# Three modulation vectors of the second layer moved from the first FFN to the second mixer, FFN steps issued one at a time, and one activation-table load instead of three

## The chip, the core and the metric

The kernel runs on one core of one Trainium2 chip. The number that counts is the device time of one execution in microseconds (us); three runs of the kernel before the change are the base. The engines are named as in the profile: PE does the matrix products and PEld loads its weights, DVE is the vector engine, ACT the scalar (activation) engine, POOL a further vector engine that is nearly idle here, and SP issues most of the DMAs.

## What is computed

Two layers of a diffusion backbone over 512 latent and 256 context tokens of width 1024. What matters here:

```python
for l in range(2):
    m_lat = split(silu(c)     @ mod_w[l] + mod_b[l], 6)   # mod_w[l]: 1024 x 6144
    m_ctx = split(silu(c_ctx) @ mod_w[l] + mod_b[l], 6)
    h = modulate(rms(x) , m[0], m[1])                     # shift, scale
    o = _even_mixer(h) if l == 0 else _odd_mixer(h)       # GLA + attention | HGRN2
    x = x + m[2] * rms(o @ w_out)                         # gate
    h = modulate(rms(x), m[3], m[4])
    x = x + m[5] * rms(swiglu(h))                         # hidden width 2816
```

Each layer needs six modulation vectors of 1024 numbers, for the latent and for the context stream. In layer 1 only the latent stream goes on after the mixer, so its vectors 2 to 5 are needed for one stream alone. In the code a vector and stream is written as a pair (m, r): r is 0 for the latents and 1 for the context. Layer 0's mixer has forget gates whose log-sigmoid needs `exp` and `ln` on ACT; layer 1's mixer has learned lower bounds (a softmax over two rows, computed once and early).

## The kernel before

Every float32 operand is split into a high and a low part (`wH`, `wL`; `x` stands for both parts of the activations), and every product is three matmuls (`mm3`, L371). A weight slab of 512 KB goes through a DMA into `raw`, a cast on ACT (`wH`, L698 and L753) and a subtraction on DVE (`wL`, L699 and L754). The order of each engine's instructions is found by the framework's scheduler when the kernel is built, except in parts that are pinned to the order in which they are written (layer 0's mixer and the heads of layer 1's mixer are, the first FFN and the values of the second mixer are not).

**Modulation vectors.** `mod_vec` is a generator that other loops advance. A step loads one slab `mraw` (128 rows of `mod_w` by 1024, 512 KB) and DVE adds it, weighted by one number per row, to an accumulator `macc` (L551 for the first row block, L553 for the other seven); where a job holds a vector for both streams, one slab is added to two accumulators. When a job's eight row blocks are through, four matmuls add up the partitions (`mod_acc`, L371), DVE copies the sums (`modrows`, L485), PE turns them with four transposes (`modT`, L374), and DVE adds the bias (`modcol`, L497). A job with a gate also makes a row of it (`gc` L599, transpose `gcT`, `gt` L605, a small DMA).

**The first FFN** (about 440 to 940 us of the span) runs gate and up projections as a block scheme of seven products (`seven`: the bank `ab` and the tiles `E` and `D` take the results, and DVE folds them into `go` and `uo` at L825, L832, L834, L835), and the down projection in parts (`acc_part`: `acc` is added to `y` at L846). Its function `fill` advances the FFN's modulation generator by one `yield`: twice in every product `seven`, once for every token tile of `acc_part`. That generator (`late_mods`) has five jobs: layer 0's gate 5, layer 1's vectors 0 and 1 (each for both streams), and layer 1's vectors 2 to 5 for the latents.

**The second mixer** begins with the values: x times the part of `odd_w_in` that starts at column 3 D, in column blocks of 256. Two blocks are done while the FFN ends. The other two, c0 = 512 and 768, are the loop at the head of `odd_mixer`; `odd_values` does three pairs of token tiles each (576 `nat` matmuls in all). Then come the heads (`ff` is their first product).

**The activation table.** `gla_gates` runs twice in layer 0's mixer and begins with a request for the table with `exp` and `ln` (L1218). The lower bounds (`lower_bounds`, L454) run before it and cause a load of their own.

Of the kernel before, what the change touches and what calls it, by code (L numbers as in the profile page):

```python
# [18 lines left out]
D = 1024  # L19
# [11 lines left out]
R_C, R_CC, R_NPM, R_MB, R_NQM, R_NPF, R_NQF, R_BG, R_LB, R_GG, R_HG, R_END = 0, 8, 16, 32, 128, 144, 160, 176, 180, 212, 213, 214  # L31
# [102 lines left out]
class Attention:  # L134
# [66 lines left out]
    def turned(self, p, dsts, vector, scratch=False):  # L201

        nc, net = self.nc, self.net
        for b, dst in enumerate(dsts):
            m = dst.shape[1]
            pt = net.sc_tile("pT", self.other()) if b and scratch else net.tr_tile("pT")
            for i in range(m):
                net.tr(pt[:, i * P : (i + 1) * P], p[:, (4 * b + i) * P : (4 * b + i + 1) * P], net.ident)
            src = pt[:, : m * P].rearrange("p (c i) -> p c i", c=m)
            (nc.vector.tensor_copy if b in vector else nc.scalar.copy)(dst, src)  # L210
# [19 lines left out]
    def rows(self, t):  # L230
        nc, net = self.nc, self.net
        pr = net.tr_tile("rB")
        for j in range(4):
            for n in range(2):
                hd = 4 * n + j
                net.mm(
                    pr[self.half[n], P * j : P * j + P],
                    self.r[t][:, hd : hd + 1].to_broadcast([P, 64]),
                    net.ident,
                    start=True,  # L240
                    stop=True,
                    tile_position=(0, 64 * n),
                )
        w = net.wp.tile([P, WU], F32, tag="mraw", bufs=2, name="o")
        nc.scalar.copy(w[:, :512], pr)
        self.o[t] = w[:, :512], w[:, 512:]
# [93 lines left out]
class Net:  # L340
# [187 lines left out]
        yield  # L528
        turned()

    def mod_vec(self, pool, jobs, own=None, bufs=2, sums=2):


        nc = self.nc
        steps = [(l, k, m) for l, ms, _ in jobs for k in range(KD) for m in sorted({m for m, _ in ms})]
        load = lambda l, k, m: self.mod_loads(l, (m,), k, own, bufs)[0]
        u = load(*steps[0])
        i = 0
        for l, ms, then in jobs:
            self.mod_tiles(l, [m for m, r in ms if r == 0])  # L540
            accs = [pool.tile([P, D], F32, tag="macc", bufs=sums, name=f"macc{l}{m}{r}") for m, r in ms]
            while i < len(steps) and steps[i][0] == l and steps[i][2] in [m for m, _ in ms]:
                k, m = steps[i][1:]
                i += 1
                ahead = load(*steps[i]) if i < len(steps) else None
                for a, (mm, r) in zip(accs, ms):
                    if mm != m:
                        continue
                    w = self.scT[:, k, r : r + 1]
                    if k == 0:  # L550
                        nc.vector.tensor_scalar(a, u, w, None, op0=ALU.mult)  # L551
                    else:
                        nc.vector.scalar_tensor_tensor(a, u, w, a, op0=ALU.mult, op1=ALU.add)  # L553
                u = ahead
                yield

            yield
            acc = self.tr_tile("mod_acc")
            for j in range(4):
                self.mm(  # L560
                    acc[32 * j : 32 * j + 32, :],
                    self.one.to_broadcast([P, 32]),
                    accs[j // 2][:, (j % 2) * 512 : (j % 2) * 512 + 512],
                    start=True,
                    stop=True,
                    tile_position=(0, 32 * j),
                )
            turned = self.mod_cols(l, acc, 512, [(m, r, 0, 2 * n, 0, 2) for n, (m, r) in enumerate(ms)])
            yield
            turned()  # L570
            if then:
                rows = self.gate_rows(l, *then)
                yield
                rows()
# [482 lines left out]
    def even_mixer(self, h, mix, zu, last):  # L1057
        nc, I = self.nc, self.I
        w = I["even_w_in"][0]
# [32 lines left out]
        def decays():  # L1092
# [7 lines left out]
            for c in range(2):  # L1100
                yield from self.gla_gates(mixg, tp, c, zT, wg, fs[c])

        self.lower_bounds()
        mods = self.mod_vec(tp, ((0, ((2, 0), (2, 1)), (2, R_NQM)), (0, ((3, 0), (3, 1)), None)), tp, 3, 4)

# [109 lines left out]
    def gla_gates(self, mixg, tp, c, zT, wg, fs):  # L1215

        nc = self.nc
        self.tc.keep_in_program_order(nc.scalar.preload_act_table_set("natural_log_exp_and_others"))  # L1218
        for t0, N in ((SEQ, CTX), (0, SEQ)):
            f = mixg.tile([P, 2, N], F32, tag=f"glaf{c}{t0}", bufs=1, name=f"glaf{c}{t0}")  # L1220
            for d in range(2):
                bias = self.col[:, R_BG + 2 * d + c : R_BG + 2 * d + c + 1]
                pt = self.sc_tile(f"logit{c}{d}")[:, :N]
                self.mm(pt, wg[:, d, c * P : (c + 1) * P], zT[:, t0 : t0 + N], start=True, stop=True)
                am = tp.tile([P, 2, SEQ], F32, tag="am", bufs=2, name="am")
                a, m = am[:, 0, :N], am[:, 1, :N]
                nc.scalar.activation(a, pt, AF.Abs, bias=bias)
                nc.scalar.activation(a, a, AF.Exp, scale=-1.0)
                nc.scalar.activation(a, a, AF.Ln, bias=self.one)
                nc.vector.tensor_scalar(m, pt, bias, 0.0, op0=ALU.add, op1=ALU.min)  # L1230
                nc.vector.tensor_tensor(m, m, a, op=ALU.subtract)
                nc.scalar.activation(f[:, d, :], m, AF.Exp, scale=1.0 / 16.0)
                if d:
                    fs.append(f)
                yield
# [96 lines left out]
    def odd_mixer(self, h, fi):  # L1332
        nc, I = self.nc, self.I
        w = I["odd_w_in"][0]
        for c0 in range(512, D, 256):
            self.odd_values(fi, h, c0, (4, 0, 2))

        with self.pool("hg") as gp:
            ones = gp.tile([P, CTX], F32, tag="ones", name="ones")
# [283 lines left out]
    def run(self):  # L1623
        nc, I, out = self.nc, self.I, self.out
# [17 lines left out]
        h = Split(ha)  # L1642
        with self.pool("pre0") as pp:
# [18 lines left out]
            for half in range(2):  # L1662
# [26 lines left out]
                for r, tok in ((1, slice(512, 768)), (0, slice(0, 512))):  # L1689
                    for k in range(ks.start, ks.stop):  # L1690
                        x = xT[:, k, tok]
# [52 lines left out]
        def late_mods(pool):  # L1744
            return self.mod_vec(
                pool,
                (
                    (0, ((5, 0), (5, 1)), (5, R_NQF)),
                    (1, ((0, 0), (0, 1)), None),
                    (1, ((1, 0), (1, 1)), None),  # L1750
                    (1, ((2, 0), (3, 0)), (2, R_NQM, 1)),
                    (1, ((4, 0), (5, 0)), (5, R_NQF, 1)),
                ),
            )

        def ending(ys):
# [19 lines left out]
            return ender(ep, 0, 5, order, xat(x1), only_lat(xat(x2)), (1, 1, 0, R_NPM), h1), values(), ep  # L1776

        ys = self.ffn(0, ha, yp, fp, pp, rp, forms, ending, late_mods)
        fp.release()

# [73 lines left out]
```

## Time and profile before

| | |
|---|---|
| median of 3 runs | 1752.65 us (1751.57 to 1753.44) |
| the profiled execution | 1750.86 us, of which the span of the core is 1749.1 us |
| granted PE clock, mean | 0.994 |
| PE busy | 1700.5 us, 97% of the span |
| PEld busy | 1524.9 us, 87% |
| DVE busy | 1276.7 us, 73% |
| ACT busy | 858.2 us, 49% |
| DMA | 187.23 MB, mean 107 GB/s |

The span is the time from the first to the last recorded instruction; 1.76 us of the profiled execution lie around it. PE works almost all the time, so what a change gains or costs is to be looked for in the moments in which PE does not work, and in the work that it is given.

### The profile page before, as it was taken

The page shows a single profiled execution, that of the slowest core. Times are in us where ns is not written, and L with a number is a line of the kernel's source. Part 1 is how long each engine was busy: PE and PEld are TensorE (multiplying, and loading weights), DVE is VectorE, ACT ScalarE, POOL GpSimd, SP SyncE. Part 2 cuts the span into 40 slices and gives each one's busy share as a digit, 9 for nine tenths or more (in the row PEclk, how much of TensorE's full clock was granted, in tenths as well). Part 3 has the DMA queues.
Part 4 walks back from the last instruction along what each step waited for, and adds up shares of the span by engine and source line. Part 5 has one row for each costly group of instructions (what it writes and reads, how often), then busy time and mean ns, then how long its engine had stood idle before and what let it go on. Part 6 is the DMA issues. An engine that isn't in the chain of part 4 may idle for free. (4 is left out here: it accounts for less than half of the span.)

```text
span 1749.1 us, 32748 instructions
## 1 busy us (share of the span) xinstructions
PE 1700.5 (97%) x13720; PEld 1524.9 (87%) x13720; DVE 1276.7 (73%) x2035; ACT 858.2 (49%) x1475; POOL 74.0 (4%) x93
## 2 busy tenths in 40 slices
PE   6999999999999999999999999999999999999998
PEld 4888986778998889898998998889898898899997
DVE  5879658735969999796668328787764678878785
ACT  5545557736542233333346436666644654444342
POOL 1004100001000000000001000000000000000000
PEclk8999999999999999999999999999999999999999
DMA  8731013154324465452225222121124333233333
GB/s 318 221 112 39 3 38 107 34 156 141 119 85 145 133 192 170 134 179 61 73 85 180 85 61 63 48 62 50 50 62 133 121 103 99 88 107 105 94 106 120
DMA packets 169647, 187.23 MB, mean 107 GB/s; under 512 B 6262, under 2 KB 140956, under 8 KB 169500
## 3 DMA queue, kind: packets, MB, share of 16 engines
q1 hardware_dynamic: 167568, 181.56, 33.0%
q10 hardware_dynamic: 1932, 3.59, 0.6%
q8 instruction: 107, 1.75, 0.4%
q14 instruction: 40, 0.33, 0.1%
HBM read 175.66 MB, written 9.46 MB: 106 GB/s over the span
## 5 line engine op out<-in xcount | busy, mean ns | idle before, releaser
L699 DVE TENSOR_TENSOR wL<-raw,wH 128x1024 fp32r<-128x1024 f32 (+1 forms) x126 | 151.3, 1207 | 115.7 <-ACT wH L698 115.4
L371 PE MATMUL nat<-wH,x 128*128 128x256 f32 (+1 forms) x1216 | 228.5, 287 | 0.0
L753 ACT CAST wH<-raw 128x1024 fp32r<-128x1024 f32 x120 | 124.6, 1052 | 176.6 <-PE acc L371 82.8
L371 PEld LDWEIGHTS nat<-wH,x 128*128 128x128 f32 x1216 | 193.2, 193 | 2.3 <-ACT natq L1115 0.8
L754 DVE TENSOR_TENSOR wL<-raw,wH 128x1024 fp32r<-128x1024 f32 x120 | 145.3, 1221 | 62.9 <-ACT wH L753 62.8
L698 ACT CAST wH<-raw 128x1024 fp32r<-128x1024 f32 (+1 forms) x126 | 128.9, 1039 | 113.3 <-PE nat L371 35.8
L371 PE MATMUL nat<-wL,x 128*128 128x256 f32 (+1 forms) x608 | 173.4, 285 | 0.0
L371 PE MATMUL acc<-wH,gH 128*128 128x512 f32 x440 | 172.6, 393 | 0.0
L371 PE MATMUL acc<-wH,gL 128*128 128x512 f32 x440 | 171.7, 390 | 0.0
L371 PE MATMUL acc<-wL,gH 128*128 128x512 f32 x440 | 171.5, 390 | 0.0
L846 DVE TENSOR_TENSOR y<-y,acc 128x1024 f32<-128x1024 f32 x135 | 114.9, 862 | 31.5 <-PE acc L371 28.2
L371 PE MATMUL ff<-x,wH 128*128 128x512 f32 (+1 forms) x512 | 127.6, 340 | 0.0
L553 DVE SCALAR_TENSOR_TENSOR macc<-mraw,scT,macc 128x1024 f32<-128x1024 f32 x98 | 122.6, 1278 | 4.7 <-DMA mraw<-in_mod_w_dram 4.5
L623 POOL TENSOR_TENSOR rs<-ms,neghalf 128x1 f32<-128x1 f32 (+2 forms) x62 | 58.0, 937 | 1597.5 <-DVE ms L621 1597.4
L371 PEld LDWEIGHTS nat<-wL,x 128*128 128x128 f32 x608 | 117.3, 193 | 0.0
L371 PE MATMUL oproj<-wH,x 128*128 128x512 f32 x320 | 102.7, 398 | 2.4 <-ACT x L1269 2.4
L371 PEld LDWEIGHTS acc<-wH,gH 128*128 128x128 f32 x440 | 82.6, 188 | 19.7 <-issue 2.5
L371 PEld LDWEIGHTS acc<-wH,gL 128*128 128x128 f32 x440 | 82.6, 188 | 17.4
L371 PEld LDWEIGHTS acc<-wL,gH 128*128 128x128 f32 x440 | 82.7, 188 | 16.1
L371 PEld LDWEIGHTS ff<-x,wH 128*128 128x128 f32 x512 | 87.3, 190 | 10.0
L954 ACT COPY qkh<-arr 128x512 f32<-128x512 f32 x112 | 70.0, 642 | 36.5 <-DVE arr L959 32.2
L371 PE MATMUL ff<-x,wL 128*128 128x256 f32 (+1 forms) x256 | 86.2, 337 | 0.0
(345 smaller groups left out, 4046.2 us busy)
## 6 DMA issues: line engine op xcount, KB each, us to landing
mraw<-in_mod_w_dram SPq DMA_DIRECT2D x96, 512.0 KB, 4.4
raw<-in_ffn_w_gate_dram SPq DMA_DIRECT2D x44, 512.0 KB, 3.8
raw<-in_ffn_w_up_dram SPq DMA_DIRECT2D x44, 512.0 KB, 3.9
raw<-in_ffn_w_down_dram SPq DMA_DIRECT2D x44, 512.0 KB, 3.6
raw<-in_odd_w_in_dram SPq DMA_DIRECT2D x40, 512.0 KB, 3.8
raw<-in_even_w_in_dram SPq DMA_DIRECT2D x16, 512.0 KB, 4.4
x<-xr SPq DMA_DIRECT2D x14, 512.0 KB, 2.6
xr<-x SPq DMA_DIRECT2D x14, 512.0 KB, 3.6
```

The costliest lines, as they stand in the source:

```text
L371: return self.pin(self.nc.tensor.matmul(*a, **k))
L553: nc.vector.scalar_tensor_tensor(a, u, w, a, op0=ALU.mult, op1=ALU.add)
L623: nc.gpsimd.tensor_tensor(rs, ms, self.neghalf.to_broadcast([P, w]), op=ALU.pow)
L698: nc.scalar.copy(H[:, :m], raw[:, :m])
L699: nc.vector.tensor_tensor(L[:, :m], raw[:, :m], H[:, :m].bitcast(F32), op=ALU.subtract)
L753: self.nc.scalar.copy(H, f)
L754: self.nc.vector.tensor_tensor(L, f, H.bitcast(F32), op=ALU.subtract)
L846: nc.vector.tensor_tensor(y, y, pt, op=ALU.add)
L954: nc.scalar.copy(qkv[:, :, :, half, :], dst)
```

## The change

Four things change.

1. `mod_vec` gets a switch `single`. With it, a row block that is added to two accumulators takes two `yield`s, one for each addition; without it both additions stand in one.
2. The first FFN's generator loses layer 1's vectors 2, 3 and 4 and is run with `single`. It has four jobs instead of five, 32 slab loads instead of 56, 56 additions on DVE instead of 80, and 66 `yield`s instead of 69; `fill` is called 90 times. A job with one vector computes its sums twice over, so it still has four `mod_acc` matmuls.
3. The three vectors are made in `odd_mixer`, among the blocks c0 = 512 and 768 of the values: five `yield`s after each pair of token tiles, with four buffers for slabs and three accumulators in a pool of their own.
4. The request for the table moves from `gla_gates` to the line ahead of `lower_bounds`.

```diff
-    def mod_vec(self, pool, jobs, own=None, bufs=2, sums=2):
+    def mod_vec(self, pool, jobs, own=None, bufs=2, sums=2, single=False):
...
-                for a, (mm, r) in zip(accs, ms):
-                    if mm != m:
-                        continue
+                here = [(a, r) for a, (mm, r) in zip(accs, ms) if mm == m]
+                for x, (a, r) in enumerate(here):
+                    if x and single:
+                        yield
                     w = self.scT[:, k, r : r + 1]
...
-                    accs[j // 2][:, (j % 2) * 512 : (j % 2) * 512 + 512],
+                    accs[j // 2 % len(accs)][:, (j % 2) * 512 : (j % 2) * 512 + 512],
...
+        self.tc.keep_in_program_order(nc.scalar.preload_act_table_set("natural_log_exp_and_others"))
         self.lower_bounds()
...
     def gla_gates(self, mixg, tp, c, zT, wg, fs):
         nc = self.nc
-        self.tc.keep_in_program_order(nc.scalar.preload_act_table_set("natural_log_exp_and_others"))
...
     def odd_mixer(self, h, fi):
+        lp = self.open_pool("late")
+        late = self.mod_vec(lp, ((1, ((2, 0), (3, 0)), (2, R_NQM, 1)), (1, ((4, 0),), None)), lp, 4, 3)
         for c0 in range(512, D, 256):
-            self.odd_values(fi, h, c0, (4, 0, 2))
+            us = self.nat_units(w, 3 * D + c0, 256, 0) + self.nat_units(w, 3 * D + c0, 256, 1)
+            for t0 in (4, 0, 2):
+                self.odd_values(fi, h, c0, (t0,), us)
+                for _ in range(5):
+                    next(late, None)
+        for _ in late:
+            pass
+        lp.release()
...
                     (0, ((5, 0), (5, 1)), (5, R_NQF)),
                     (1, ((0, 0), (0, 1)), None),
                     (1, ((1, 0), (1, 1)), None),
-                    (1, ((2, 0), (3, 0)), (2, R_NQM, 1)),
-                    (1, ((4, 0), (5, 0)), (5, R_NQF, 1)),
+                    (1, ((5, 0),), (5, R_NQF, 1)),
                 ),
+                single=True,
```

The orders that result are shown at three places. The lines of the new kernel are one to ten higher than those of the old one for the same statement.

On DVE, in a product `seven` of the first FFN, the old order has the additions in pairs between a product's folds (L825, L832) and the weight splits (L754).

```order
L553 SCALAR_TENSOR_TENSOR macc_6091<-mraw_6111,scT,macc_6091 128x1024
L553 SCALAR_TENSOR_TENSOR macc_6092<-mraw_6111,scT,macc_6092 128x1024
L754 TENSOR_TENSOR wL<-raw,wH 128x1024
L553 SCALAR_TENSOR_TENSOR macc_6091<-mraw_6131,scT,macc_6091 128x1024
L553 SCALAR_TENSOR_TENSOR macc_6092<-mraw_6131,scT,macc_6092 128x1024
L825 TENSOR_TENSOR uo<-uo,ab 128x384
L553 SCALAR_TENSOR_TENSOR macc_6091<-mraw_6189,scT,macc_6091 128x1024
L553 SCALAR_TENSOR_TENSOR macc_6092<-mraw_6189,scT,macc_6092 128x1024
L754 TENSOR_TENSOR wL<-raw,wH 128x1024 x2
L832 TENSOR_TENSOR uo<-uo,E 128x384
```

In the new order a product `seven` in the same part of the FFN, one in which a job ends, reads as follows (L778 adds weight blocks, its new line is L779; L846 is now L847).

```order
L755 TENSOR_TENSOR wL<-raw,wH 128x1024 x2
L779 TENSOR_TENSOR raw<-raw 128x512 x2
L552 TENSOR_SCALAR macc_7736<-mraw_7593,scT 128x1024
L485 COPY modrows<-mod_acc 128x512
L826 TENSOR_TENSOR uo<-uo,ab 128x384
L755 TENSOR_TENSOR wL<-raw,wH 128x1024
L554 SCALAR_TENSOR_TENSOR macc_7736<-mraw_7737,scT,macc_7736 128x1024
L497 TENSOR_TENSOR modcol_7105<-modT,col 128x8 x2
```

Six of the rows shown of the old order are additions, two of those of the new one. The copy of a finished job's sums stands ahead of the fold L826 in three of the four jobs.

On PE, at the end of the values, the old order goes straight from the last `nat` matmul to the first head's product.

```order
L371 MATMUL nat<-wH,x_9413 128x256
L371 MATMUL nat<-wL,x_9413 128x256
L371 MATMUL nat<-wH,x_9414 128x256
L371 MATMUL ff_10368<-x_9411,wH 128x256
L371 MATMUL ff_10368<-x_9412,wH 128x256
L371 MATMUL ff_10368<-x_9411,wL 128x256
```

The new order has the last job's sums and their transposes between them.

```order
L371 MATMUL nat<-wH,x_9311 128x256
L371 MATMUL nat<-wL,x_9311 128x256
L371 MATMUL nat<-wH,x_9312 128x256
L371 MATMUL mod_acc<-macc_10238,one 32x512 x4
L374 MATMUL modT<-ident,modrows 128x128 x4
L371 MATMUL ff_10383<-x_9309,wH 128x256
L371 MATMUL ff_10383<-x_9310,wH 128x256
L371 MATMUL ff_10383<-x_9309,wL 128x256
```

The two matmul groups of vector 4 follow each other with nothing in between. The sums of vectors 2 and 3 stand 96 `nat` matmuls earlier, their transposes 16 matmuls behind them and the gate's transpose another 8 behind. On SP the 24 slab loads stand in one block behind the weights of the values and the first head's first weights, and ahead of all other weights of the heads.

On ACT the two rows `L1218 ACT_TABLE_LOAD` of layer 0's mixer are gone and nothing stands in their place; the one load that is left, L1104, stands where the load of the lower bounds stood. With the shorter ACT the scheduler also changes DVE's order in layer 0's mixer. The old order there, ahead of the copy `zT` that the gates' first product reads, is this one (L466 is the last step of the lower bounds, L699 the split of the layer's input weights).

```order
L466 TENSOR_SCALAR nlb_638<-lb_636 128x16
L553 SCALAR_TENSOR_TENSOR macc_690<-mraw_846,scT,macc_690 128x1024
L553 SCALAR_TENSOR_TENSOR macc_691<-mraw_846,scT,macc_691 128x1024
L699 TENSOR_TENSOR wL<-raw,wH 128x1024
L553 SCALAR_TENSOR_TENSOR macc_690<-mraw_919,scT,macc_690 128x1024
L1098 COPY zT<-zTp 32x512
```

In the new order the same place reads as follows.

```order
L700 TENSOR_TENSOR wL<-raw,wH 128x1024
L554 SCALAR_TENSOR_TENSOR macc_691<-mraw_845,scT,macc_691 128x1024
L554 SCALAR_TENSOR_TENSOR macc_692<-mraw_845,scT,macc_692 128x1024
L554 SCALAR_TENSOR_TENSOR macc_691<-mraw_918,scT,macc_691 128x1024
L700 TENSOR_TENSOR wL<-raw,wH 128x1024
L1099 COPY zT<-zTp 32x512
```

The same work stands ahead of `zT`, but the third addition has moved ahead of the weight split. Further on, the additions up to the job's end and the copy `modrows` keep their number.

## The prediction

> **What bounds the kernel now.** I read the head of the page first, for the bound.
>
> ```profile
> span 1749.1 us, 32748 instructions
> PE 1700.5 (97%) x13720; PEld 1524.9 (87%) x13720; DVE 1276.7 (73%) x2035; ACT 858.2 (49%) x1475; POOL 74.0 (4%) x93
> ```
>
> PE is the bound with 97%. A change off PE can gain only what PE waits for that engine, and each matmul that it adds is paid in full. Next come the groups and the DMA issues, for the price of what moves.
>
> ```profile
> L553 DVE SCALAR_TENSOR_TENSOR macc<-mraw,scT,macc 128x1024 f32<-128x1024 f32 x98 | 122.6, 1278 | 4.7 <-DMA mraw<-in_mod_w_dram 4.5
> ```
>
> ```profile
> mraw<-in_mod_w_dram SPq DMA_DIRECT2D x96, 512.0 KB, 4.4
> ```
>
> One addition is 1.28 us of DVE, and a slab needs 4.4 us from issue to landing. Then the table of windows: first layer 0's mixer, then three parts of the first FFN (additions dense, fewer, none), last the values of the second mixer. The columns are window, length, then busy time and instructions of PE, PEld, DVE, ACT and POOL, granted PE clock, DMA share and GB/s.
>
> ```profile
> 50.00:110.00 60.00, 58.06 (x394) 50.92 (x393) 57.05 (x75) 32.55 (x54) 0.00 (x0) 1.00 0.63 193
> 440.00:660.00 220.00, 217.01 (x1158) 199.23 (x1158) 197.05 (x232) 81.64 (x112) 0.00 (x0) 1.00 0.44 137
> 660.00:820.00 160.00, 158.32 (x829) 143.35 (x828) 134.43 (x172) 55.90 (x77) 0.00 (x0) 1.00 0.45 142
> 820.00:930.00 110.00, 109.36 (x577) 102.02 (x577) 71.83 (x88) 41.84 (x57) 0.00 (x0) 1.00 0.31 99
> 982.00:1030.00 48.00, 48.00 (x400) 48.00 (x401) 5.77 (x5) 10.23 (x15) 0.00 (x0) 1.00 0.16 45
> ```
>
> DVE is nearly full in layer 0's mixer (57.05 of 60 us), at 90%, 84% and 65% in the parts of the FFN, and at 12% in the values, where PE has no gap: 400 instructions in 48 us, 0.12 us each. Last the waits of PE, from 440 to 930 us and then from 48 to 125 us: what was waited for, total, number and longest.
>
> ```profile
> PE ab L371 <- DVE uo L825: 2.4, 3, 1.1
> PE ab L371 <- ACT go L817: 1.9, 2, 1.4
> PE ab L371 <- DVE go L825: 0.9, 2, 0.6
> ```
>
> ```profile
> PE modT L374 <- DVE modrows L485: 1.5, 1, 1.5
> PE logit L371 <- issue: 0.4, 1, 0.4
> ```
>
> In the whole FFN PE waits 5.2 us in seven places. That is all a lighter DVE can give back there, and 1.9 us in layer 0's mixer.
>
> **Part 1: the first FFN loses 24 additions and one job.** How an addition becomes a wait is seen on DVE ahead of the wait at 646.92 us, and then on PE.
>
> ```profile
> 641.56 1.29 DVE L553 SCALAR_TENSOR_TENSOR macc<-mraw,scT,macc 128x1024 f32<-128x1024 f32 x1 [1.41 <-DMA mraw<-in_mod_w_dram]
> 642.76 1.22 DVE L754 TENSOR_TENSOR wL<-raw,wH 128x1024 fp32r<-128x1024 f32 x1
> 643.90 1.28 DVE L553 SCALAR_TENSOR_TENSOR macc<-mraw,scT,macc 128x1024 f32<-128x1024 f32 x1
> 645.09 1.22 DVE L754 TENSOR_TENSOR wL<-raw,wH 128x1024 fp32r<-128x1024 f32 x1
> 646.23 0.55 DVE L825 TENSOR_TENSOR uo<-uo,ab 128x384 f32<-128x384 f32 x1
> ```
>
> ```profile
> 646.92 0.59 PE L371 MATMUL ab<-T,wH 128*128 128x384 f32 x2 [1.08 <-DVE uo L825]
> ```
>
> The fold L825 frees the bank `ab`; it stands behind two additions, of which the first waited 1.41 us for its slab, and PE waits 1.08 us for it. With half the additions in front this wait would go. But there is one of the same kind where no addition is left:
>
> ```profile
> 852.11 0.62 PE L371 MATMUL ab<-T,wH 128*128 128x384 f32 x2 [0.64 <-DVE go L825]
> ```
>
> So not all waits are the additions' doing. The bounds are 0 and 5.2, and about 0.1 for each of seven restarts, 5.9 us. Two estimates lie between. By density, with the list of waits taken part by part; this is the part from 660 to 820 us:
>
> ```profile
> PE ab L371 <- DVE uo L825: 1.3, 2, 0.9
> PE ab L371 <- DVE go L825: 0.2, 1, 0.2
> ```
>
> The shares of DVE, 90%, 84% and 65%, go with waits of 3.0 us in 220 (the rest of the 5.2), 1.5 in 160 and 0.6 in 110 (the one at 852.11), that is 1.4, 0.9 and 0.55 in 100 us. Without 24 x 1.28 = 30.7 us, DVE's 331.5 us of the first 380 become 301, or 79%. There the rate would be about 0.85, 3.2 us in 380 instead of 4.5, a gain of 1.3. By place: the waits at 646.92 and the two for `go` of L817, 3.0 us together, have additions on DVE in the 10 us ahead. I take 2.0 us, between the two. That `single` puts one addition in a slot where two stood works on these same 5.2 us, so it has no term of its own.
>
> On PE the lost job counts in full. A job among the products of `acc`:
>
> ```profile
> 527.05 0.39 PE L371 MATMUL acc<-wH,gL 128*128 128x512 f32 x1
> 527.37 1.06 PE L371 MATMUL mod_acc<-macc,one 128*32 128x512 f32 x8
> 528.36 0.50 PE L371 MATMUL acc<-wH,gH 128*128 128x512 f32 x1
> ```
>
> ```profile
> 530.99 0.40 PE L371 MATMUL acc<-wH,gL 128*128 128x512 f32 x1
> 531.22 0.60 PE L374 MATMUL modT<-ident,modrows 128*128 128x128 f32 x4
> 531.58 0.47 PE L371 MATMUL acc<-wH,gH 128*128 128x512 f32 x1
> ```
>
> From the start of the `acc` matmul before it to the start of the one behind it, 528.36 - 527.05 = 1.31 us, of which 0.23 is the usual pitch of `acc` (530.99 to 531.22), and 0.11 the slower restart behind it (0.50 against 0.39): 1.08 + 0.11 = 1.19 us for the sums. The transposes come to 0.36 + 0.09 = 0.45 us in the same way, and the gate's one transpose to a quarter of that, 0.1. A job with a gate is 1.74 us: minus 1.7.
>
> **Part 2: the values get two jobs.** PE has no gap there, so the same prices are added: with a gate 1.74, without 1.64, together 3.4 us. DVE has room: 24 x 1.28 = 30.7 us in a stretch in which it works 12%. What PE waits for, though, is new. At the end of the values `modT` follows `mod_acc` at once and needs the copy `modrows`. How long that takes is seen at the FFN's last job, on PE and on DVE.
>
> ```profile
> 806.20 1.07 PE L371 MATMUL mod_acc<-macc,one 128*32 128x512 f32 x8
> 807.20 0.62 PE L371 MATMUL E<-x,wH 128*128 128x384 f32 x2
> ```
>
> ```profile
> 807.34 0.69 DVE L485 COPY modrows<-mod_acc 128x512 f32<-128x512 f32 x1 [2.71 <-PE mod_acc L371]
> ```
>
> The copy ends at 808.03, and PE could go on at 807.20: 0.8 to 0.9 us idle. I take 0.9, with 0 and one more addition ahead of the copy (2.2) as ends. The transposes of vectors 2 and 3 stand 16 matmuls behind their sums, 1.9 us, which covers the copy's 0.83; the gate's transpose has 8 matmuls, 1.0 us, against two `modcol` adds and `gc`, and may find an addition of 1.28 in front: 0.3, between 0 and 1.3. Sum 3.4 + 0.9 + 0.3 = 4.6.
>
> The slabs: 24 loads go through four buffers; a buffer turns in 4.4 + 1.28 = 5.7 us, so one slab comes every 1.4 us, and 16 of them need 23 us. The two blocks last 288 x 0.12 = 34.6 us, the sums of vectors 2 and 3 are asked for 96 x 0.12 = 11.5 us before their end, at 23 us, and the first additions can run before the blocks begin. It fits with little to spare. On SP the loads stand ahead of the heads' second weights. The 24th slab is issued when the 20th is used up, 20 x 1.4 = 28 us after the first, which is some 10 us ahead of the end of the values; the weights then need 4 us to land and 2.5 us for cast and split, and the first head product (9 us by the timeline) covers them a second time. It costs nothing unless the slabs are over 12 us late. The pool that holds the slabs is given back when the last sums are through; what uses its room next is the heads' work on DVE and POOL behind the first head product, 9 us later.
>
> **Part 3: the tables.** ACT loses two loads in layer 0's mixer, the second of which shows the price, and DVE waits there for ACT.
>
> ```profile
> 81.95 0.78 ACT L1134 COPY gqk<-gqk 128x768 f32<-128x768 f32 x1
> 82.75 1.28 ACT L1218 ACT_TABLE_LOAD   x1
> 84.05 0.84 ACT L1227 ACTIVATE am<-logit,col 128x256 f32<-128x256 f32 x2
> ```
>
> ```profile
> 91.41 1.30 DVE L1231 TENSOR_TENSOR am<-am 128x512 f32<-128x512 f32 x2 [0.65 <-ACT am L1229]
> ```
>
> ```profile
> 64.85 1.23 DVE L699 TENSOR_TENSOR wL<-raw,wH 128x1024 fp32r<-128x1024 f32 x1 [1.15 <-ACT wH L698]
> 65.99 1.28 DVE L553 SCALAR_TENSOR_TENSOR macc<-mraw,scT,macc 128x1024 f32<-128x1024 f32 x1
> 67.19 1.00 DVE L1098 COPY zT<-zTp 32x512 f32<-32x512 f32 x2
> ```
>
> The load is 1.28 us, and the next instruction starts 1.30 us behind its start. ACT is half idle, so the 2.6 us count only through DVE: its idle 0.65 us goes, and with the addition ahead of the split the 1.15 us at 64.85 are filled and `zT` comes up to 1.15 us earlier, which ends the wait of `logit`. All the additions up to `modrows` then end up to 1.8 us earlier, and PE's 1.5 us for `modT` shrink. The bounds are 0 and 1.9; since the slabs of DVE's additions may not come earlier by as much, I take two thirds, minus 1.3.
>
> The Trainium skill ("ScalarE: Activation LUTs", What ACT_TABLE_LOAD costs) puts a load at about 1283 ns and a drain of about 1380 ns beside it, 2.66 us for a switch to a different set. By that ACT would lose 5.3 us instead of 2.6. Here the load agrees, but the row ahead ends at 82.73 and the one behind starts at 84.05, which leaves no room for the drain; this load asks for the set that is there already, so no row here shows a switch for the drain to be seen in. The term would stay within the same bounds, 0 to 1.9.
>
> **The sum.** 4.6 - 1.7 - 2.0 - 1.3 = -0.4 us. The profiled execution took 1750.86 us (1749.1 and 1.76 around it), 1.8 less than the median; on the median, 1752.65 - 0.4 = 1752.2 us. This measurement can tell about 0.2%, 3.5 us, from no change.
>
> **The rivals.**
>
> *Faster: the waits of the FFN all go.* For it speaks that six of the seven lie where additions are, against it the wait at 852.11. FFN minus 5.9, layer 0's mixer minus 1.9, lost job minus 1.7, values plus 4.6: minus 4.9, 1747.7 us.
>
> *Slower: the slabs come late in the values.* The place is the sums of vectors 2 and 3, which PE reaches 23 us into the blocks. DVE's order holds two weight splits among the first ten additions, and behind a split that waits for ACT the slabs that have landed keep their four buffers. If a slab takes 1.65 us instead of 1.4, the sixteenth is 4 us late, and PE stands still for 4 us: 1756 us. It decides from 3.9 us of lateness. For it speaks the 1.41 us that an addition waited for its slab at 641.56; against it the DMA share of 0.16 in the values against 0.44 in the FFN.
>
> *The additions are not what PE waits for.* Then the FFN's waits stay, since what frees `ab` late is the weight splits' place: plus 2.0 on the forecast, 1754.2 us, within the bound. The wait at 852.11 speaks for it, the one at 646.92 against it.
>
> **How the numbers follow.** The forecast has a chance of 0.54, the faster rival 0.20, the slower one 0.13, waits that stay 0.13. From the forecast's own spread (plus or minus 2.5 us by the bounds of its terms) 0.04 goes to faster, and 0.04 of the third case to slower: faster 0.24, same 0.59, slower 0.17. The range from 1746.5 to 1757.5 holds the faster and the slower rival with about 1 us beyond each.
>
> **What would show it.** In the FFN, the list of PE's waits should hold three to four us instead of 5.2, the one at 646.92 gone. In the values, two groups `mod_acc` of 1.1 us, the second followed by 0.9 us idle of PE ahead of `modT` with DVE `modrows` as the releaser; an idle PE ahead of the first `mod_acc` would be the slower rival. In layer 0's mixer, no wait for `logit` and less than 1 us for `modT`. I am wrong if the FFN's waits rise, which would mean that the changed order, and not the load, sets them.

## The result, and the profile after

The changed kernel takes 1749.21 us (median of 10 runs, 1746.00 to 1751.86) against 1751.37 us before (10 runs, 1750.22 to 1755.05): ratio 0.9982, 95% interval 0.9973 to 0.9990, or about 3 us less, with 1.5 either way. The ratios in this document are estimated from all runs of both kernels; they are not the quotient of the two medians, which here differ by 2.2 us. A second measurement gave 0.9993 (0.9983 to 1.0003; 1751.80 against 1752.19 us). The forecast was 1752.2 on a base of 1752.65, so minus 0.4; the time lies inside the range, and the small gain lies at the edge of what a measurement can tell.

The page's head shows the bound unchanged. PE has 12 instructions more, and the 24 additions are still there, only elsewhere.

```profile
span 1747.5 us, 32790 instructions
PE 1700.9 (97%) x13732; PEld 1526.0 (87%) x13732; DVE 1280.9 (73%) x2036; ACT 857.8 (49%) x1473; POOL 74.2 (4%) x93
```

The table of windows, same stretches and columns as before:

```profile
50.00:110.00 60.00, 58.48 (x399) 51.37 (x398) 57.10 (x75) 28.89 (x52) 0.00 (x0) 1.00 0.62 192
440.00:660.00 220.00, 220.00 (x1178) 204.51 (x1177) 177.42 (x213) 86.91 (x117) 0.00 (x0) 1.00 0.33 103
660.00:820.00 160.00, 158.50 (x826) 143.47 (x825) 132.01 (x164) 51.57 (x70) 0.00 (x0) 1.00 0.36 110
820.00:930.00 110.00, 109.72 (x583) 102.40 (x582) 73.95 (x94) 44.81 (x63) 2.03 (x3) 1.00 0.32 102
982.00:1030.00 48.00, 46.32 (x382) 43.98 (x382) 32.17 (x34) 10.68 (x14) 0.32 (x1) 1.00 0.75 249
```

From 440 to 660 us PE has no gap left, and DVE fell from 90% to 81%. In the values DVE went from 12% to 67%, the DMA share from 0.16 to 0.75, and PE now stands still there. PE's waits from 440 to 930 us:

```profile
PE ab L371 <- ACT go L818: 0.8, 1, 0.8
PE ab L371 <- DVE go L826: 0.6, 2, 0.3
PE ab L371 <- DVE uo L826: 0.3, 1, 0.3
```

5.2 us in seven waits have become 1.7 in four. From 48 to 125 us and then from 984 to 1031 us:

```profile
PE modT L374 <- DVE modrows L485: 1.5, 1, 1.5
```

```profile
PE modT L374 <- DVE modrows L485: 0.9, 1, 0.9
PE modT L374 <- DVE pr L1375: 0.8, 1, 0.8
```

The wait for `logit` is gone, the one for `modT` in layer 0's mixer is just what it was, and two new ones of the same kind stand in the values. The second is put down to a small MEMSET that ended last by the profile; the timeline of DVE has `modrows` ending at the same moment.

Where the time went, and for all kernels that follow, is read from four marks in the timeline of PE: the start of the span, the first product of the first FFN, the 288th `nat` matmul from the end (the beginning of the blocks c0 = 512 and 768), the first `ff`. The orders of all engines behind the last mark are the same in all these kernels, but for a row or two at the mark. The last column holds PE's waits from 440 to 930 us; from there to the end of the FFN PE waits another 1.3 to 2.8 us, of which 0.2 to 1.5 us are for a tile `hf` that ACT makes.

| kernel (one profiled execution each) | to the FFN | FFN | values | rest | span | PE's waits in the FFN |
|---|---|---|---|---|---|---|
| before | 424.2 | 570.5 | 34.6 | 719.8 | 1749.1 | 5.2 |
| after | 423.7 | 564.9 | 39.8 | 719.2 | 1747.5 | 1.7 |
| after, second profile | 423.5 | 563.6 | 39.4 | 721.1 | 1747.7 | 2.2 |
| e1 tables alone | 423.6 | 570.0 | 34.6 | 722.2 | 1750.4 | 5.1 |
| e2 late vectors alone | 424.1 | 566.3 | 39.6 | 721.1 | 1751.1 | 3.6 |
| e3 single steps alone | 426.5 | 569.8 | 34.6 | 722.6 | 1753.4 | 6.1 |
| e4 two late vectors | 423.7 | 564.3 | 36.4 | 722.9 | 1747.4 | 2.0 |
| e5 eight table loads | 424.1 | 570.9 | 34.6 | 726.1 | 1755.6 | 6.0 |
| e6 six steps a pair | 424.0 | 564.0 | 41.2 | 719.5 | 1748.6 | 1.8 |
| e7 two slab buffers | 423.6 | 564.3 | 62.3 | 724.5 | 1774.7 | 1.9 |
| e8 after, tables as before | 425.0 | 566.7 | 39.4 | 720.7 | 1751.9 | 3.4 |
| e9 e4, transposes apart | 421.9 | 566.8 | 36.4 | 719.2 | 1744.4 | 2.9 |
| e10 after, 49 additions left out | 423.2 | 565.5 | 40.2 | 721.2 | 1750.2 | 2.5 |
| e12 e9 in pairs | 421.8 | 567.6 | 36.4 | 720.3 | 1746.1 | 4.4 |

The rest, whose code no kernel changes, takes anything from 719.2 to 726.1 us. So the total of one execution can't tell 1 us. A stage tells more, but it varies too where the order of instructions is the same: the FFN took from 563.6 to 566.7 us in five executions of the changed kernel's order (after twice, e6, e7, e8), and the stage up to the FFN from 424.1 to 426.5 us in four executions of the old order (before, e2, e3, e8). The granted clock in the FFN was 1.00 in all of them.

### The profile page after: what moved, and what is told of

It is laid out like the page before. It is cut to its first block, busy times and chain, and to the rows that moved or that the text cites. A ratio compares the mean times of both kernels' runs of the same rounds, so it can differ in the third digit from the quotient of the medians.

```text
span 1747.5 us, 32790 instructions
## 1 busy us (share of the span) xinstructions
PE 1700.9 (97%) x13732; PEld 1526.0 (87%) x13732; DVE 1280.9 (73%) x2036; ACT 857.8 (49%) x1473; POOL 74.2 (4%) x93
## 3 DMA queue, kind: packets, MB, share of 16 engines
q8 instruction: 107, 1.75, 0.4%
## 5 line engine op out<-in xcount | busy, mean ns | idle before, releaser
L754 ACT CAST wH<-raw 128x1024 fp32r<-128x1024 f32 x120 | 124.5, 1051 | 197.2 <-PE acc L371 86.2
L699 ACT CAST wH<-raw 128x1024 fp32r<-128x1024 f32 (+1 forms) x126 | 128.9, 1038 | 127.8 <-PE nat L371 34.4
L847 DVE TENSOR_TENSOR y<-y,acc 128x1024 f32<-128x1024 f32 x135 | 115.2, 863 | 37.0 <-PE acc L371 32.8
```

The costliest lines, as they stand in the source:

```text
L699: nc.scalar.copy(H[:, :m], raw[:, :m])
L754: self.nc.scalar.copy(H, f)
L847: nc.vector.tensor_tensor(y, y, pt, op=ALU.add)
```

## The experiments

**Tables, late vectors and single steps, each alone.** The four kernels of this group ran on one chip beside the same 28 runs of before.

e1 moves the request for the table and nothing else:

```diff
+        self.tc.keep_in_program_order(nc.scalar.preload_act_table_set("natural_log_exp_and_others"))
         self.lower_bounds()
...
     def gla_gates(self, mixg, tp, c, zT, wg, fs):
         nc = self.nc
-        self.tc.keep_in_program_order(nc.scalar.preload_act_table_set("natural_log_exp_and_others"))
```

> The kernel before with the table request moved alone (one table load instead of three). Theory A (a table load costs the kernel only what DVE is held up by it, and DVE's other waits take most of that place): layer 0's mixer ends 0.2 to 0.4 us earlier, as in the changed kernel, PE's wait for modT stays at 1.4 to 1.6 us, total 0.3 us below before, not to be told from it. Theory B (the term of the prediction): the wait for modT shrinks below 1 us, total 1.3 us below before.

Measured: ratio 0.9986 (0.9977 to 0.9995); the stage up to the FFN 0.6 us shorter, PE's wait for `modT` 1.5 us as ever. PE's wait for `logit` stayed too, 0.5 us. Of the 0.6 us, 0.2 are there by the transposes `modT` (108.7 us against 108.9); the rest goes with a wait of 0.4 us for `pcg`, at 167.8 us in before, which comes and goes with either order (0.4 in the second profile of the changed kernel, none in e5). The stage speaks for theory A. The total fell by 2.4 us with 1.6 either way, more than the stage shows, and what it has beyond that stands in no stage that the change touches; that part stays open.

e2 moves the three vectors but keeps pairs and tables:

```diff
-                single=True,
...
     def gla_gates(self, mixg, tp, c, zT, wg, fs):
         nc = self.nc
+        self.tc.keep_in_program_order(nc.scalar.preload_act_table_set("natural_log_exp_and_others"))
```

(shown against the changed kernel, together with the request ahead of `lower_bounds`, which goes).

> The three vectors are made in the second mixer, but the first FFN keeps its additions in pairs and the tables stay as before. Theory L (what PE waits for in the FFN is DVE's load, which falls by 24 additions): the waits of PE in the FFN fall to 1 to 2.5 us as in the changed kernel (1.7), total 0 to 1 us above the changed kernel, about 1749.5. Theory S (it is the spacing, two additions in a row, that makes PE wait): the waits stay at 4 to 6 us and the total is 3 to 4 us above the changed kernel, 1752.5 to 1753, since the values' added 5.3 us are paid in both.

Measured: ratio 1.0002 (0.9991 to 1.0013), waits 3.6 us, between the theories. The list of waits shows what stayed; the row of PE's timeline behind it is the longest.

```profile
PE ab L371 <- ACT go L818: 1.9, 2, 1.4
PE ab L371 <- DVE go L826: 1.7, 3, 1.1
```

```profile
562.63 0.44 PE L371 MATMUL ab<-x,wH 128*128 128x384 f32 x1 [1.38 <-ACT go L818]
```

Before has the same two waits for ACT's `go`, 1.9 us together, 1.4 the longest, at the same place (562.39 us). These are the rows of DVE and ACT there, in before:

```profile
560.55 3.67 DVE L553 SCALAR_TENSOR_TENSOR macc<-mraw,scT,macc 128x1024 f32<-128x1024 f32 x3
560.92 1.04 ACT L698 CAST wH<-raw 128x1024 fp32r<-128x1024 f32 x1 [1.73 <-issue]
561.87 0.47 ACT L817 COPY go<-ab 128x384 f32<-128x384 f32 x1
```

The copy `go` that frees `ab` stands behind a cast of a weight block on ACT and starts 0.95 us after it. Three additions stand in a row on DVE at that moment, but they run until 564.22 us, when PE's wait is long over; at most the first can have had a share. At the second wait (610.82 us in before) the copy starts 0.94 us after such a cast again, at 610.29, and the next addition comes only at 611.09. In the changed kernel ACT makes the same copy at 555.84 us, and the cast comes behind it, at 558.63. The waits for `uo` are gone in e2, with the additions that stood in front of them. What the late vectors give in the FFN, 4.2 us, the values take back with 5.1.

e3 gives the old jobs single steps and changes nothing else:

```diff
                     (1, ((4, 0), (5, 0)), (5, R_NQF, 1)),
                 ),
+                single=True,
```

> The kernel before with the additions one to a slot and nothing else: all five jobs and 80 additions stay in the first FFN, nothing is added to the values. Theory S (spacing): PE's waits in the FFN fall to 1 to 2.5 us, total 2.5 to 4 us below before, about 1748, better than the changed kernel. Theory L (load): the waits stay at 4 to 6 us, total within 1 us of before, about 1751.5.

Measured: ratio 0.9988 (0.9978 to 0.9998), waits 6.1 us. In the waits theory S fell.

```profile
PE ab L371 <- ACT go L818: 3.3, 4, 1.8
PE ab L371 <- DVE go L826: 2.8, 2, 2.0
```

The waits of the dense first part went, but 80 single steps fill the slots to the FFN's end, and new waits came from 750 to 894 us, where before had few additions or none. The total is lower all the same, by more than this profile shows; that is not explained.

e4 keeps two late vectors and gives the third back to the FFN:

```diff
-        late = self.mod_vec(lp, ((1, ((2, 0), (3, 0)), (2, R_NQM, 1)), (1, ((4, 0),), None)), lp, 4, 3)
+        late = self.mod_vec(lp, ((1, ((2, 0), (3, 0)), (2, R_NQM, 1)),), lp, 4, 2)
...
-                    (1, ((5, 0),), (5, R_NQF, 1)),
+                    (1, ((4, 0), (5, 0)), (5, R_NQF, 1)),
```

> The changed kernel, but vector 4 goes back to the first FFN, into the job that computed vector 5's sums twice; the values keep vectors 2 and 3 (16 slabs, one job). PE then loses a whole job in the values (1.64 us) and the wait of 0.81 us for its modrows at their end; the first FFN gets 8 more additions and no more work on PE. If the FFN's waits stay at about 2 us, total 2 to 2.5 us below the changed kernel, about 1747. Under theory L they rise by some 0.5 us, and the gain is 1.5 to 2; if the FFN's waits come back to 4 us or more, the total equals the changed kernel's.

Measured: 1749.32 against 1754.96 us, ratio 0.9969 (0.9957 to 0.9980). The values take 1.8 us more than before, one job with a gate (1.74 by the prediction's prices) and no wait, and the FFN keeps its gain with 2.0 us of waits. Up to the first `ff` its profile takes 1024.4 us, against 1029.3 before and 1028.4 and 1026.6 in the two profiles of the changed kernel. The jobs that summed one vector twice were a whole job's PE time for nothing.

**Prices and floors.** The next four ran beside 27 runs of before.

e5 asks for the table ahead of every gate logit:

```diff
                 pt = self.sc_tile(f"logit{c}{d}")[:, :N]
                 self.mm(pt, wg[:, d, c * P : (c + 1) * P], zT[:, t0 : t0 + N], start=True, stop=True)
+                self.tc.keep_in_program_order(nc.scalar.preload_act_table_set("natural_log_exp_and_others"))
                 am = tp.tile([P, 2, SEQ], F32, tag="am", bufs=2, name="am")
```

(the request at the head of `gla_gates` goes).

> The kernel before with a table request ahead of every gate logit, eight loads instead of two in layer 0's mixer, so 6 x 1.28 = 7.7 us more of ACT there. Theory A (a load costs only what DVE is held up by it): ACT's own queue is half idle, layer 0's mixer gets 0 to 1.5 us longer up to modT, total 0 to 2 us above before. Theory B (the term of the prediction, two loads are worth 1.3 us): 4 us above before. By the drain of the Trainium skill (a switch to a different set) nothing more would show, since every load after the first asks for the set that is there.

Measured: ratio 0.9994 (0.9985 to 1.0003); to the FFN 424.1 us, as before with 424.2. PE's waits from 48 to 125 us show what happened on the way.

```profile
PE logit L371 <- issue: 1.3, 1, 1.3
PE modT L374 <- DVE modrows L485: 0.9, 1, 0.9
PE logit L371 <- DVE am L1230: 0.2, 1, 0.2
```

PE waits 1.1 us longer for `logit` than in before and 0.6 us less for `modT`, and the stage ends when it did. Six more loads cost nothing there, so two fewer can't be worth 1.3 us by their own length; theory B fell. The profiled execution itself is long because of the rest, 726.1 us.

e6 takes six steps behind each pair:

```diff
-                for _ in range(5):
+                for _ in range(6):
```

> The changed kernel with six steps behind each pair of token tiles instead of five, so that the last job ends one pair earlier and its transposes no longer follow its sums at once. The wait of 0.81 us for modrows at the end of the values goes. PE reaches the sums of vectors 2 and 3 about 5.8 us earlier, at about 1005.9 us, and those of vector 4 at about 1020; in the changed kernel the last additions they need ended at about 1005.2 and 1019.8. If the slabs keep that pace, total 0.8 us below the changed kernel, values 39.0 us instead of 39.85; if they come later by 1 us or more, PE waits at the sums and the gain is gone.

Measured: ratio 0.9990 (0.9981 to 0.9998), values 41.2 us instead of 39.4 to 39.8. PE did not wait at the sums, so the slabs were not late for them. What was held up is the gate's transpose:

```profile
PE gcT L374 <- DVE gc L600: 2.2, 1, 2.2
PE modT L374 <- DVE pr L1375: 0.7, 1, 0.7
```

`gc` stood behind three additions, 3.9 us from 1011.68 us on, for which PE waited 2.2 us, and the wait that was to go stayed at 0.7: its `modrows` now stands behind a weight split (`wL`, 1021.92 us, 1.23 us).

e7 gives the slabs two buffers:

```diff
-(1, ((4, 0),), None)), lp, 4, 3)
+(1, ((4, 0),), None)), lp, 2, 3)
```

> The changed kernel with two buffers for the late slabs instead of four. Theory of the slower rival: a slab then comes every 2.9 to 3.4 us (5.7 to 6.8 us for a buffer's turn, over two) instead of 1.8, the 16th addition ends some 48 us or more after the first, at about 1024 us, and PE waits at the first sums for 10 us or more; the total rises by 10 to 25 us over the changed kernel. If the additions' pace were set by DVE's weight splits and not by the slabs, the total would stay within 2 us of the changed kernel.

Measured: 1775.41 against 1754.12 us, ratio 1.0115 (1.0101 to 1.0129), values 62.3 us.

```profile
PE mod_acc L371 <- DVE macc L554: 18.3, 3, 13.8
```

The slower rival's mechanism is real, and in the changed kernel it is some way off: there the 16th addition ended at about 1005 and PE asked for it at 1011.67 us. The 24 additions took from 975.6 to 1019.8 us, 1.8 us each and not the 1.4 of the prediction.

e8 is the changed kernel with the tables as before (the diff of e2 in `gla_gates` alone, single steps kept).

> The changed kernel with the table requests left where they were before (three loads): late vectors and single steps together. The first FFN's waits should be those of the changed kernel, 1.5 to 2.2 us, against 3.6 with the late vectors alone and 6.1 with the single steps alone: the two work only together. Total: by theory A (tables worth 0.3 us) 0.3 us above the changed kernel, about 2 us below before; by theory B 1.3 us above the changed kernel, about 1 us below before.

Measured: ratio 0.9999 (0.9987 to 1.0010), waits in the FFN 3.4 us with the very order of the FFN on all engines that had 1.7 to 2.2 in four other executions (after twice, e6, e7). Its longest wait, 1.72 us at 750.08, stands behind an addition that waited 1.75 us for its slab; in the first profile of after that addition waited 0.88. "The two work only together" was too strong: one order gives between 1.7 and 3.4. And e8 differs from e2 in `single` alone: waits of 3.4 against 3.6 us, an FFN of 566.7 against 566.3, ratios of 0.9999 and 1.0002. In this pair `single` gave nothing that could be measured.

**The transposes, the floor, and the result again.** The last but one group ran beside 17 runs of before.

e9 is e4 with one pair of token tiles between a job's sums and its transposes in layer 0's mixer, and one ahead of the gate's transpose:

```diff
-        ... v0 m m kv q m m q m q m m m m m m m m m qk1 kv m")
+        ... v0 m m kv q m q m q m m m m m m m m m m qk1 kv m")
```

> The kernel with two late vectors (e4) and, in layer 0's mixer, one pair of token tiles' matmuls put between the sums of the first job (mod_acc) and their transposes (modT), and another ahead of the gate's transpose. If PE waits 1.5 us there only because the transposes follow at once, as at the end of the values, that wait goes and the total is 1.5 us below e4, some 6 to 7 us below before. If the wait is the lateness of DVE itself, it reappears at the transposes of the second job, and the total equals e4's.

Measured: 1746.31 against 1752.19 us, ratio 0.9965 (0.9952 to 0.9978); to the FFN 421.9 us, 1.8 less than e4.

```profile
112.84 0.28 PE L371 MATMUL nat<-wH,x 128*128 128x256 f32 x1
112.96 0.60 PE L374 MATMUL modT<-ident,modrows 128*128 128x128 f32 x4
113.32 0.36 PE L371 MATMUL nat<-wH,x 128*128 128x256 f32 x1
```

The transposes start at the usual pitch, without a wait, and none comes back at the second job: with 48 matmuls between the two groups the 1.5 us are gone. That the total is better than e4's is not shown. The intervals of the two ratios lie almost wholly over each other, and in the profile the FFN took 566.8 us against e4's 564.3 with the same order of instructions, so that up to the first `ff` e9 needed 1025.1 us and e4 1024.4.

e10 leaves out 49 of the 56 additions of the changed kernel's first FFN (slabs and matmuls stay):

```diff
                     if k == 0:
                         nc.vector.tensor_scalar(a, u, w, None, op0=ALU.mult)
-                    else:
+                    elif not skip:
                         nc.vector.scalar_tensor_tensor(a, u, w, a, op0=ALU.mult, op1=ALU.add)
...
                 single=True,
+                skip=True,
```

> The changed kernel, leaving out of the first FFN all additions but the first of each accumulator (7 of the 56 stay), while the slabs are still loaded and the matmuls and transposes stay. If all waits of PE in the FFN are the additions' doing, they fall from 1.7 to 3.4 us below 0.5 us. If what is left in the changed kernel belongs to the weights (third rival), they stay at 1 to 2 us.

Measured: one run, 1752.01 us; waits 2.5 us. All four are waits for DVE's fold `go`. The changed kernel has two of these, at 798.06 and 844.63 us, 0.6 us together, with no addition close in front of them on DVE; so they are not the additions' doing. The changed kernel's longest, 0.84 us at 746.87 for ACT's `go`, is gone in e10; with the additions it stands behind one that waited 0.88 us for its slab. (With the additions left out the scheduler also places some rows of PE and DVE a little differently.) DVE ahead of e10's longest, 1.12 us at 846.55:

```profile
PE ab L371 <- DVE go L826: 2.5, 4, 1.1
```

```profile
842.88 0.69 DVE L779 TENSOR_TENSOR ws<-raw 128x512 f32<-128x512 f32 x1 [2.19 <-DMA raw<-in_ffn_w_up_dram]
843.61 0.69 DVE L779 TENSOR_TENSOR raw<-raw 128x512 f32<-128x512 f32 x1
844.22 1.82 DVE L1554 TENSOR_TENSOR gL<-uo,gH 128x768 fp32r<-128x768 f32 x2
845.95 0.54 DVE L826 TENSOR_TENSOR go<-go,ab 128x384 f32<-128x384 f32 x1
```

The fold that frees `ab` stands behind a weight block that waited 2.19 us for its DMA. The changed kernel has the same rows ahead of its wait at 844.63, with 1.34 us for the DMA. That is the third rival's case, as a floor of about 2 us. A fourth buffer for `raw` would test it; it wasn't tried.

The changed kernel was then run once more:

> The changed kernel once more, on the same chip as the two-vector kernel's variant and beside the same runs of before: how much of the difference is the chip's. From the traces (first FFN 5.5 us shorter, values 5.1 us longer, layer 0's mixer 0.6 to 1.1 us shorter) the total should be 1 to 1.5 us below before, ratio 0.9992; by the first measurement 0.9982.

Measured: 0.9993 (0.9983 to 1.0003), which the traces' 1 to 1.5 us fit better than the first 0.9982 does; the two intervals overlap.

**Pairs or single steps at the same load.** e12 is e9 without `single`, beside 15 runs of before on its chip:

> The best kernel so far (two late vectors, transposes apart: e9) with the additions of the first FFN in pairs again, 64 of them. If single steps matter for themselves, the waits behind three additions in a row come back, the one of 1.4 us at about 560 us and the one of 0.5 at about 609, which stood in all four traces with pairs, and PE's waits in the FFN are 4 to 5 us against 2.9 in e9; total 1 to 2 us above e9. If only the number of additions matters, the waits stay at 2 to 3.4 us and the total equals e9's.

Measured: 1749.82 against 1753.63 us, ratio 0.9979 (0.9970 to 0.9988), waits 4.4 us against 2.9 in e9.

```profile
560.48 0.61 PE L371 MATMUL ab<-x,wH 128*128 128x384 f32 x2 [1.38 <-ACT go L818]
```

```profile
PE ab L371 <- DVE go L826: 2.0, 3, 1.5
PE ab L371 <- ACT go L818: 1.9, 2, 1.4
PE ab L371 <- DVE uo L826: 0.5, 1, 0.5
```

The wait of 1.38 us, and the one of 0.5 us 48 us later, stand in all five profiles with pairs and in none with single steps. So these two waits, 1.9 us, belong to the order that pairs bring. It isn't the three additions in a row: e9 has three in a row too, from 607.90 us, without such a wait. What goes with them is ACT's order: in the five profiles with pairs a weight cast stands right in front of the copy `go`, at both places, and in the nine with single steps the copy that frees `ab` near 560 us comes ahead of the cast. What `single` is worth in all is not shown: the sum of the waits differs by 1.5 us here and the FFN by 0.8, less than one order varies by (e8), and the totals' intervals overlap.

## Why the prediction was right, and where it was not

**Layer 0's mixer, minus 1.3.** The wrong mechanism. The wait for `modT` did not shrink in any kernel with the load moved, until e9 and e12 put other matmuls ahead of it (in e5 it was 0.9 us, behind a longer wait for `logit`). DVE's old idle time went, but the new order puts the gates' steps earlier, and DVE waits there for ACT and for the logits instead; up to `modrows` it gained 0.26 us. The stage up to the FFN is 423.2 to 424.0 us in the seven profiles with one load (e9 and e12 left aside) and 424.1 to 425.0 in the others, with 426.5 in e3: 0.7 us between the means without e3, 1.2 with it, so the size stays open. The wait for `logit` is the one that was seen to shrink: 0.4 to 1.1 us in before, e2, e3 and e8, none in five of the seven, but still 0.5 in e1 and e4.

**The first FFN, minus 2.0 and minus 1.7.** The direction held and the first term was too small. The changed order's FFN took 564.9, 563.6, 564.0, 564.3 (e7) and 566.7 us, 564.7 on average; the old one's 570.5, 570.0 and 570.9, 570.5. That is 5.8 us less. The lost job has 1.7 of it by the prediction's price, and the listed waits, from 5.4 to 2.2 us on average, have 3.2 and not 2.0; about 1 us stands in no listed wait and is not accounted for. The mechanism held in part. With the late vectors alone (e2) the waits fell from 5.2 to 3.6 us, near the forecast, and the waits for `uo` went. The two waits for ACT's `go`, 1.9 us, were put down to additions in the estimate by place, and wrongly: they stay with 56 additions (e2) and with 64 (e12), and what stands ahead of the copy is a cast on ACT itself. They went with the order that `single` brings, so that `single` "has no term of its own" was wrong as a mechanism; how much time the new order gives in all stays open, since other waits took their place in e3 and e8. The third rival was right on part of what remains: e10 has hardly an addition and waits 2.5 us.

**The values, plus 4.6.** Measured 39.4 to 39.8 against 34.6, plus 4.8 to 5.3. The matmuls' 3.4 and the 0.9 at the end held (0.8); the first job's transposes, which 16 matmuls were to cover, waited 0.5 to 0.9 us, since `modrows` stood behind additions that waited for slabs; the gate's transpose did not wait. The slabs' price was wrong: the additions took 1.8 us each, beyond the 1.65 from which the slower rival had PE stand still. PE did not, since the first addition ran at 975.6 us, 12.9 us ahead of the blocks; the prediction names such a start, but has no number for it.

```profile
1011.67 1.06 PE L371 MATMUL mod_acc<-macc,one 128*32 128x512 f32 x8
1015.70 0.66 PE L374 MATMUL modT<-ident,modrows 128*128 128x128 f32 x4 [0.86 <-DVE modrows L485]
```

**The sum.** By stages, minus 0.7, minus 5.8 and plus 5.1: minus 1.4 us, against minus 0.4 forecast; the FFN gave 2.1 us more than forecast, the values cost 0.5 more and the mixer gave 0.6 less. That the sum came so near is in part luck: errors of 2.1 and of 1.1 us stood against each other, and the mixer's term came from a wait that did not move. Of the measured totals, minus 1.2 with 1.8 either way holds the 1.4; minus 3.1 with 1.5 does not, though nearly. What the first has beyond it is not accounted for by any stage.

**The rivals.** The faster one had the right place (the waits) but not the floor. The slower one was shown by e7 to be a real mechanism; with four buffers PE did not wait for the sums, not even in e6, which asks for them earlier.

## What to carry to other kernels

Work that is moved off a busy engine to one that has room still costs its part on the engine that bounds the kernel: here the values gave back 5.1 of the 5.8 us, and the gain came when that part was not doubled (e4). Two groups on the bounding engine with a short step of another engine between them want other matmuls between them; moving them apart ended a wait of 1.5 us (e9). Where the order is found by a scheduler, a change on one engine moves rows on the others as well: what stood ahead of the copy that frees a bank was a cast on ACT, though the edit was about additions on DVE (e12). And before more load is taken away it pays to run the kernel without it once and see what waits remain (e10).

## What was not expected of the hardware

Loading again the table set that is already there cost nothing that could be measured: eight loads in layer 0's mixer took no longer up to the FFN than two (424.1 and 424.2 us), though each load takes 1.28 us on ACT; what PE waited longer for `logit`, 1.1 us, it waited less later. And code that no kernel changed took between 719.2 and 726.1 us over the profiled executions, a wider spread than any term of this prediction (several chips had a share in them). Most of that goes with two things the traces show. The granted PE clock of this stretch, averaged, was 0.990 in e5 (726.1 us), 0.995 in before (719.8) and 0.998 in e6 (719.5), and PE's waits in it were 13.9, 10.5 and 10.9 us; in the second FFN, those for `go` of L817 were 4.9 us in the profile of before and 6.4 in e5's. If the waits and the share of the clock that was not granted are taken off, an estimate, 704.5 to 706.9 us are left in all fourteen profiles.
